# A reciprocal of 16 softmax denominators leaves the step that transposes them and becomes a step of its own

## The chip, the cores and the metric

The kernel runs on one core of a Trainium2 chip. The metric is the device time of one execution in microseconds (us), the median of several runs.

## The reference

One inference step of a two-layer decoder trunk, for a prompt of 1024 tokens and a sample group of 8 x 4 tokens that share the weights. Layer 0 projects its input once and feeds two mixers: a gated depthwise convolution of width 31, and attention with 16 heads of 64. Layer 1 is a gated linear recurrence. In the prompt's attention a head attends under three (window, dilation) pairs, and the three outputs are merged by their softmax denominators:

```python
DSWA_CONFIGS = ((128, 1), (512, 4), (2048, 16))
...
    scores = jnp.where(mask[None, None, :, None, :, :], scores, -jnp.inf)
    lse = jax.nn.logsumexp(scores, axis=-1)
    p = jnp.exp(scores - lse[..., None])
    o = jnp.einsum('ndbhqk,ndbkhe->ndbqhe', p.astype(vv.dtype), vv)
...
def dswa_merge(parts):
    outs = jnp.stack([o for o, _ in parts], axis=0).astype(jnp.float32)
    lses = jnp.stack([l for _, l in parts], axis=0)
    w = jax.nn.softmax(lses, axis=0)
    return jnp.einsum('cnth,cnthe->nthe', w, outs)
```

That merge equals one softmax over all keys, each counted as often as the three windows hold it. The kernel computes it so: a mask adds the logarithm of the count, one exponential is taken, its sum over the keys is the denominator, and the output is divided by it at the end.

## The kernel before

The program is generated by a planner written in Python that emits every engine's instructions in an order of its own and holds a clock for each engine (`clk`). The spine is a list of dense jobs (`dense`): each multiplies one 128-column block of a weight with all tokens in three chunks of 384, 384 and 288, in fp32 split into high and low halves, 24 matmuls for a chunk. They go into three PSUM tiles named d, and VectorE or ScalarE evacuates them.

All other work is in threads, lists of atoms (steps). An atom has an engine ("kind"), a set of keys that it depends on, a key that it sets when it ends, and a claim on buffers. A thread's atoms are issued strictly in their order. After every three dense matmuls `sides()` goes through the threads by priority (attention has 2, the convolution's taps 5) and issues what may go. For a TensorE atom the planned end of all that it depends on must lie 300 ns back (LEAD), a PSUM tile x must be free, and neither ScalarE's nor VectorE's planned clock may be more than 1500 ns ahead of TensorE's. For an atom of another engine that engine's planned clock may be at most 800 ns ahead (QUEUE):

```python
                if a.kind == "pe":
                    ok = r <= now + LEAD and self.xrel[0] <= now + 60 and max(c["act"], c["dve"]) <= now + 1500
                else:
                    ok = r <= max(now, c[a.kind]) + 60 and c[a.kind] <= now + QUEUE and (not a.bulk or c["dma"] <= now + 3000)
```

On the chip each engine works through its own queue in the order of issue and waits on semaphores.

`attention(pr)` makes the thread of one pair of heads, eight in all. For the blocks i = 0 to 7 of 128 queries: `qk(i)` multiplies (PSUM tiles x), a custom VectorE instruction adds the mask and finds the extreme, and ScalarE takes the exponential; its accumulated sums go into one column each of `den` (128 queries x 16, a column for each head and block). `tr` and `far` transpose the exponentials, `pv` and `far_pv` multiply with the values into PSUM tile o; `far_pv(1)` is the last of them, 32 matmuls and one copy by ScalarE into `S["o"]`. Then `fin1` takes the reciprocal of `den` on VectorE, transposes it on TensorE into 16 rows, and copies the rows out of PSUM on ScalarE; `fin2` and `fin3` write them to DRAM and read them back broadcast; `fin4` multiplies the output by them on GpSimd; `fin5` stores it for the gate.

Between a pair's `fin1` and the next pair's `qk(0)` lies a stretch of dense jobs alone. Beside attention, VectorE works on the 26 taps that it has of each of the 8 convolution blocks (scalar_tensor_tensor of 128x1024), on evacuations of d and x, and on the rotary additions. After attention, from 768 us on, come the decode attention over the cached keys and values (thread `dec`, whose bulk loads are paced by the planner's DMA clock), the layer norm and gates of layer 0, its output projection, and layer 1.

All calls go through a proxy, so the profile gives line 157 for nearly every instruction; they are told apart by engine, operation and form.

Of the kernel before, what the change touches and what calls it, by code (L numbers as in the profile page):

```python
# [176 lines left out]
class Kern:  # L177
# [786 lines left out]
    def attention(self, pr):  # L964
        nc, A = self.nc, self.A
        S = self.pair[pr]
# [116 lines left out]
        atoms = [Atom(store, "sp", [("rk", pr, c) for c in range(3)] + [("rq", pr, c) for c in range(3)], ("ko", pr))]  # L1083
        K = lambda n, i: (n, pr, i)
        for i in range(9):
# [3 lines left out]
            if i:  # L1089
# [5 lines left out]
                if t % 4 == 3:  # L1095
                    atoms.append(Atom(far_pv(t // 4), "pe", [K("pv", t)] + [K("far", x) for x in range(max(2, t - 3), t + 1)],
                                      K("fp", t // 4)))

        def fin1():
            den = S["den"]  # L1100
            nc.vector.reciprocal(den[:, :16], den[:, :16])
            p = self.px()
            nc.tensor.transpose(p[0:16, 0:128], den[:, :16], self.ident)
            S["d2"] = A.alloc(128)
            nc.scalar.copy(S["d2"][0:16, :].rearrange("p (a r) -> p r a", r=4),
                           p[0:16, 0:128].rearrange("p (r a) -> p r a", r=4))
            den.free()
            for n in ("q", "k", "vt", "vf"):
                S[n].free()
            if pr == NPAIR - 1:  # L1110
                self.mask.free()
# [15 lines left out]
        def fin5():  # L1127
            nc.sync.dma_start(self.ybd[pr][:, 0:T], S["o"].f)
            S["o"].free()
            self.fin["ob", pr] = self.clk["pe"] + 3000  # L1130

        atoms += [Atom(fin1, "pe", [("fp", pr, 1)], ("att", pr), (2, 0)), Atom(fin2, "sp"),
                  Atom(lambda: None, "sp"), Atom(fin3, "sp"), Atom(fin4, "pool"), Atom(fin5, "sp")]
        self.spawn(f"att{pr}", 2, atoms)

# [1482 lines left out]
```

## Time and profile before

| | us |
|---|---|
| median of 3 runs | 2374.55 |
| lowest and highest | 2374.27, 2379.08 |
| the profiled execution | 2373.09 |
| its span, from first to last instruction | 2371.2 |

| engine | busy us | share of the span |
|---|---|---|
| TensorE, matmuls (PE) | 2267.1 | 96% |
| TensorE, weight loads (PEld) | 2121.7 | 89% |
| VectorE (DVE) | 1617.8 | 68% |
| ScalarE (ACT) | 1025.2 | 43% |
| GpSimd (POOL) | 1055.1 | 44% |

The span is that of one execution under the hardware profiler; the profiled execution's own time is 1.9 us more. Weight loads overlap matmuls. Busy shares are averages over stages with different limits. The mean granted clock of TensorE is 0.985 of full speed.

### The profile page before, as it was taken

How to read it: one execution, taken by the hardware profiler on the slowest of the kernel's cores; microseconds unless marked ns; L12 is line 12 of the kernel's file. 1: busy time of each engine (PE TensorE's matmuls, PEld its weight loads, DVE VectorE, ACT ScalarE, POOL GpSimd, SP SyncE). 2: the span in 40 equal slices, each digit the busy share in tenths (PEclk: the TensorE clock that was granted, in tenths of full speed). 3: DMA queues.
4: the chain of work that ended last, by engine and by line, in shares of the span. 5: the costliest groups of instructions: out<-in, count | busy, mean ns of one | idle time of the engine just before them, and what ended most of it. 6: DMA issues, size and time to landing. Idle time of an engine off the chain costs nothing.

```text
span 2371.2 us, 42772 instructions
## 1 busy us (share of the span) xinstructions
PE 2267.1 (96%) x17387; PEld 2121.7 (89%) x17387; DVE 1617.8 (68%) x2466; ACT 1025.2 (43%) x1858; POOL 1055.1 (44%) x703
## 2 busy tenths in 40 slices
PE   7999999999989999999979999999999999999997
PEld 6987888887886798889969999999999999998996
DVE  7999988798786546752686666666666666667336
ACT  5454444444444322333445444444454444444332
POOL 4655555465454323434553333333333333345436
PEclk9999999999999999999989999999999999999998
DMA  4131221221235867874441111111211222232525
GB/s 151 54 95 40 77 75 40 77 75 40 77 114 210 336 246 294 296 268 138 142 165 51 67 64 64 64 64 64 73 58 64 73 73 73 74 101 98 176 96 175
DMA packets 118173, 271.60 MB, mean 115 GB/s; under 512 B 32336, under 2 KB 59472, under 8 KB 117968
## 3 DMA queue, kind: packets, MB, share of 16 engines
q1 hardware_dynamic: 117968, 268.78, 33.2%
q8 instruction: 139, 2.28, 0.4%
q14 instruction: 66, 0.54, 0.1%
HBM read 215.00 MB, written 53.73 MB: 113 GB/s over the span
## 4 chain that ended last, share of the span: by engine, by line
PE 73%; DVE 15%; issue 4%; ACT 3%; POOL 2%; DMA 2%; SPq 0%; DVEq 0%; POOLq 0%; ACTq 0%
PE d L157 41%; PE x L157 31%; DVE b L157 14%; ACT b L157 3%; POOL b L157 2%; PE o L157 1%; DVE c L157 1%; ACT c L157 0%; DMA b<-yd 0%; DMA b<-ybd 0%; DMA b<-rd 0%; DMA b<-wab 0%; SPq L157 0%; DMA b<-kc 0%; POOL c L157 0%
## 5 line engine op out<-in xcount | busy, mean ns | idle before, releaser
L157 PE MATMUL d<-c,b 128*128 128x384 f32 (+1 forms) x7896 | 1396.6, 331 | 22.1 <-ACT b L157 10.9
L157 PEld LDWEIGHTS d<-c,b 128*128 128x128 f32 x7896 | 1288.2, 190 | 69.6 <-issue 39.7
L157 POOL TENSOR_TENSOR b<-b,b 128x1024 fp32r<-128x1024 f32 (+6 forms) x422 | 845.8, 2015 | 860.8 <-ACT b L157 675.3
L157 ACT ACTIVATE b<-b 128x384 f32<-128x384 f32 (+14 forms) x647 | 357.0, 567 | 822.7 <-DVE b L157 809.9
L157 PE MATMUL x<-c,b 128*128 128x384 f32 (+4 forms) x3640 | 583.1, 311 | 26.2 <-DVE b L157 21.3
L157 PEld LDWEIGHTS x<-c,b 128*128 128x128 f32 (+2 forms) x3640 | 541.5, 175 | 43.9 <-issue 19.8
L157 DVE SCALAR_TENSOR_TENSOR b<-b,c,b 128x1024 f32<-128x1024 f32 (+2 forms) x258 | 406.5, 1578 | 10.9 <-ACT b L157 8.3
L157 DVE TENSOR_TENSOR b<-b,b 128x384 f32<-128x384 f32 (+14 forms) x297 | 303.4, 1035 | 89.8 <-ACT b L157 66.6
L157 PE MATMUL x<-b,b 128*32 128x128 f32 (+12 forms) x4528 | 281.9, 339 | 5.1 <-POOL b L157 4.3
L157 DVE SCALAR_TENSOR_TENSOR b<-b,b 128x384 f32<-128x384 f32 (+3 forms) x216 | 198.3, 924 | 107.0 <-ACT b L157 105.4
L157 PEld LDWEIGHTS x<-b,b 64*32 64x32 f32 (+3 forms) x4528 | 201.1, 127 | 56.8 <-issue 39.4
L157 DVE TENSOR_TENSOR b<-d,b 128x384 f32<-128x384 f32 (+3 forms) x278 | 139.9, 510 | 156.1 <-PE d L157 147.6
L157 ACT CAST b<-b 128x1024 fp32r<-128x1024 f32 (+3 forms) x264 | 224.7, 862 | 33.2 <-DMA b<-od 8.4
L157 DVE TENSOR_TENSOR b<-x,b 128x384 f32<-128x384 f32 (+3 forms) x162 | 81.9, 506 | 134.0 <-PE x L157 119.0
L157 POOL TENSOR_SCALAR b<-b 128x32 f32<-128x32 f32 x40 | 31.3, 782 | 288.1 <-DVE b L157 282.7
L157 ACT COPY b<-x 128x512 f32<-128x512 f32 (+4 forms) x177 | 86.4, 498 | 147.7 <-PE x L157 130.1
L157 DVE COPY b<-x 128x512 f32<-128x512 f32 (+8 forms) x216 | 100.5, 476 | 71.8 <-PE x L157 60.3
L157 ACT COPY b<-d 32x384 f32<-32x384 f32 (+2 forms) x212 | 94.7, 447 | 123.7 <-DVE b L157 80.6
L157 DVE CUSTOM_DVE_ANT_0 b<-x,b 128x128 f32<-128x128 f32 (+8 forms) x144 | 72.0, 532 | 51.9 <-PE x L157 47.7
L157 ACT ACTIVATE b<-b,c 128x512 f32<-128x512 f32 (+1 forms) x112 | 94.8, 875 | 2.6 <-DVE b L157 0.5
L157 POOL TENSOR_TENSOR b<-b,c 128x248 f32<-128x248 f32 (+1 forms) x48 | 66.8, 1406 | 36.2 <-PE d L157 33.2
L157 POOL COPY b<-b 128x32 f32<-128x32 f32 (+1 forms) x105 | 54.4, 528 | 47.8 <-DVE b L157 45.9
(59 smaller groups left out, 937.9 us busy)
## 6 DMA issues: line engine op xcount, KB each, us to landing
b<-wc SPq DMA_DIRECT2D x64, 512.0 KB, 4.2
b<-wab SPq DMA_DIRECT2D x56, 512.0 KB, 5.8
b<-kc SPq DMA_DIRECT2D x64, 448.0 KB, 6.5
b<-vc SPq DMA_DIRECT2D x64, 448.0 KB, 8.3
b<-woa SPq DMA_DIRECT2D x32, 512.0 KB, 4.2
b<-woc SPq DMA_DIRECT2D x32, 512.0 KB, 4.2
b<-yd SPq DMA_DIRECT2D x16, 528.0 KB, 6.2
ybd<-b SPq DMA_DIRECT2D x16, 512.0 KB, 3.0
```

The source lines that it names most:

```text
L157: r = f(*a, **k)
```

## The change

The reciprocal leaves `fin1` and becomes `fin0`, an atom of kind "dve". It depends on the end of `qk(7)`, stands in the thread after `far_pv(1)` and ahead of `fin1`, and sets a key that `fin1` now needs as well:

```diff
+        def fin0():
+            nc.vector.reciprocal(S["den"][:, :16], S["den"][:, :16])
+
         def fin1():
             den = S["den"]
-            nc.vector.reciprocal(den[:, :16], den[:, :16])
             p = self.px()
             nc.tensor.transpose(p[0:16, 0:128], den[:, :16], self.ident)
...
-        atoms += [Atom(fin1, "pe", [("fp", pr, 1)], ("att", pr), (2, 0)), Atom(fin2, "sp"),
+        atoms += [Atom(fin0, "dve", [("qk", pr, 7)], ("den", pr)),
+                  Atom(fin1, "pe", [("fp", pr, 1), ("den", pr)], ("att", pr), (2, 0)), Atom(fin2, "sp"),
                   Atom(lambda: None, "sp"), Atom(fin3, "sp"), Atom(fin4, "pool"), Atom(fin5, "sp")]
```

The planner's clocks see the two steps at other times than the one before, so the order of later instructions may differ too.

## Rows read from the trace of the kernel before

**Rows 1.** The page: span, and busy us, share and instructions of TensorE.

```profile
span 2371.2 us, 42772 instructions
...
PE 2267.1 (96%) x17387; PEld 2121.7 (89%) x17387; DVE 1617.8 (68%) x2466; ACT 1025.2 (43%) x1858; POOL 1055.1 (44%) x703
```

**Rows 2.** Windows: length, busy us (instructions) of PE PEld DVE ACT POOL, clock, DMA share.

```profile
66.00:768.30 702.30, 666.48 (x6150) 577.48 (x6148) 605.52 (x835) 319.05 (x698) 383.53 (x236) 0.99 0.26 80
...
235.40:330.79 95.39, 90.86 (x807) 80.45 (x808) 91.81 (x115) 43.92 (x97) 48.06 (x31) 1.00 0.21 60
330.79:421.58 90.79, 87.42 (x773) 76.96 (x774) 77.92 (x106) 41.40 (x92) 53.81 (x32) 0.98 0.22 63
421.58:507.38 85.80, 80.47 (x738) 69.77 (x739) 72.09 (x99) 36.99 (x82) 42.69 (x27) 1.00 0.23 66
507.38:596.67 89.29, 85.90 (x773) 75.42 (x774) 78.18 (x106) 41.39 (x92) 55.06 (x32) 1.00 0.21 64
596.67:682.54 85.87, 80.35 (x737) 69.64 (x738) 72.05 (x99) 37.01 (x82) 42.91 (x27) 1.00 0.22 66
```

**Rows 3.** TensorE's waits from 66 to 768.5 us: total, times, longest.

```profile
PE x L157 <- DVE b L157: 18.0, 14, 3.1
PE o L157 <- DVE b L157: 6.0, 10, 1.2
```

**Rows 4.** Groups by form, whole span: busy, mean ns, idle before, releasers.

```profile
L157 PE MATMUL x<-c,b 128*16 128x128 f32 x8 | 2.2, 269 | 14.8 <-DVE b L157 14.8
...
L157 PE MATMUL o<-b,b 128*64 128x128 f32 x608 | 49.1, 284 | 10.4 <-DVE b L157 6.0 <-ACT b L157 4.4
```

**Rows 5.** Timeline at the third pair's transpose: start, us, instruction [idle before].

```profile
321.88 1.71 PE L157 MATMUL o<-b,b 128*64 128x128 f32 x32
...
323.14 2.59 DVE L157 SCALAR_TENSOR_TENSOR b<-b,c,b 128x1024 f32<-128x1024 f32 x2
...
323.51 4.21 PE L157 MATMUL d<-c,b 128*128 128x384 f32 x27
...
326.65 1.63 DVE L157 TENSOR_TENSOR b<-b,b 128x384 f32<-128x384 f32 x1 [0.92 <-POOL b L157]
328.20 0.54 DVE L157 TENSOR_TENSOR b<-d,b 128x384 f32<-128x384 f32 x1
328.67 1.81 DVE L157 SCALAR_TENSOR_TENSOR b<-b,c,b 128x1024 f32<-128x1024 f32 x1
...
330.40 0.24 DVE L157 RECIPROCAL b<-b 128x16 f32<-128x16 f32 x1
...
330.79 0.27 PE L157 MATMUL x<-c,b 128*16 128x128 f32 x1 [3.06 <-DVE b L157]
330.81 9.25 PE L157 MATMUL d<-c,b 128*128 128x288 f32 x44
```

**Rows 6.** Timeline at the fourth pair's transpose.

```profile
415.80 3.44 DVE L157 SCALAR_TENSOR_TENSOR b<-b,c,b 128x1024 f32<-128x1024 f32 x2
...
421.58 0.27 PE L157 MATMUL x<-c,b 128*16 128x128 f32 x1 [1.61 <-DVE b L157]
```

**Rows 7.** Windows after the long waits, and the timeline after the fifth pair's.

```profile
330.81:335.01 4.20, 4.20 (x18) 4.20 (x19) 4.16 (x4) 1.72 (x5) 4.07 (x2) 0.59 0.20 62
682.57:686.77 4.20, 4.20 (x18) 4.20 (x19) 4.16 (x4) 1.72 (x5) 4.07 (x2) 0.59 0.16 58
507.40:511.60 4.20, 4.20 (x26) 4.20 (x27) 4.16 (x4) 1.71 (x5) 4.09 (x2) 1.00 0.19 66
...
507.38 0.27 PE L157 MATMUL x<-c,b 128*16 128x128 f32 x1 [2.99 <-DVE b L157]
507.40 9.28 PE L157 MATMUL d<-c,b 128*128 128x288 f32 x53
```

**Rows 8.** The decode stage: its window, and GpSimd's waits for loads of values there.

```profile
768.30:1060.00 291.70, 281.21 (x2589) 247.67 (x2590) 175.05 (x315) 94.14 (x163) 98.89 (x94) 0.98 0.77 285
...
POOL b L157 <- DMA b<-vc: 10.4, 1, 10.4
```

## The prediction

> **What bounds the kernel now.** I read the page first, then the windows, then the waits of TensorE, then the timelines of the places where the change acts. The page gives a span of 2371.2 us with TensorE busy for 2267.1 of it [rows 1]. So what counts is time in which TensorE stands still or runs at a lower clock; other engines count only where they hold it up. The profiled execution took 2373.09 us, 1.9 more than its span and 1.5 less than the median of the three runs, 2374.55; what I take off the one I take off the other.
>
> The change sits in attention, which runs from 66 to 768 us. In that stretch TensorE is busy 666.48 of 702.30 us, so it idles 35.8 us; VectorE is busy 605.52, which is 86% [rows 2]. Of TensorE's idle time, 18.0 us are waits of x matmuls (attention's PSUM tiles) for VectorE, in 14 waits of up to 3.1 us [rows 3]. The instructions by form show whose they are: the transpose of the 128x16 denominators, run eight times, once for each pair of heads, has 14.8 us of idle time before it, all put down to VectorE [rows 4], while the reciprocal that it waits for takes 0.24 us [rows 5]. The wait is therefore hardly the reciprocal; it is the place of the reciprocal in VectorE's queue.
>
> The timeline of the third pair shows this. TensorE finishes the last attention matmuls (32 of them, from 321.88), does 27 dense matmuls from 323.51 to 327.72, and then stands for 3.06 us, until the transpose at 330.79. VectorE meanwhile works through two taps of the convolution (323.14 to 325.73), a rotary addition, a PSUM evacuation and one more tap; only then, at 330.40, comes the reciprocal [rows 5]. Its input, the sums of the exponentials, is ready long before: the transposes of the last exponentials, and all that is made of them, lie ahead of the 32 matmuls.
>
> **The change part by part.** It takes the reciprocal out of fin1 and makes it a step of its own, fin0, which the planner may issue on VectorE as soon as the thread has come to it, that is right after far_pv(1) (those 32 matmuls). fin1 still waits for far_pv's copy by ScalarE, and now for fin0 too. It adds no instruction and no DMA: eight reciprocals of 0.24 us before, eight after, and eight transposes. On the queues of SP and POOL nothing is passed; the stores and loads of fin2 to fin5 follow fin1 as before.
>
> *The wait that goes.* If the reciprocal is issued after far_pv(1), it stands on VectorE behind what was issued up to then. For the third pair that is at worst the two taps that end at 325.73, so it is done by 325.97, and TensorE comes to the transpose at 327.72: 1.75 us to spare. The narrowest of the eight is the pair whose transpose starts at 421.58: two taps end at 419.24, the reciprocal would end at 419.48, and TensorE was ready at 421.58 - 1.61 = 419.97 [rows 6], with 0.49 to spare; the pair at 596.67 repeats this order. So up to 14.8 us go.
>
> *What stays of it.* The trace doesn't show a transpose whose reciprocal was issued ahead. From below the price is nothing. From above it is 0.6 us for each, the mean of the ten waits of matmuls into o for VectorE (6.0 us in all [rows 3]): 8 x 0.6 = 4.8. The nearest row is that of the o matmuls, whose operands are copied by separately issued steps, with the planner's lead, just as the reciprocal's result will be: 10.4 us of idle [rows 4] over 8 pairs x 10 steps (8 pv, 2 far_pv), 0.13 us each. I take 0.13 for six pairs and 0.6 for the two narrow ones: 2.0 us. The removal is worth 14.8 - 2.0 = 12.8 us.
>
> *The clock.* After two of the three long waits TensorE's granted clock was 0.59 of full over the next 4.20 us, and 18 matmuls ran there; after the third, 2.99 us long, it stayed at 1.00, and 26 ran [rows 7]. In the first 9.3 us after the wait that is 44 matmuls [rows 5] against 53 in 9.28 us [rows 7], of the same kind: nine fewer at 9.28/53 = 0.175 us, 1.6 us lost, twice: 3.2 us. With the waits this goes too. The bounds are 0, if a shorter wait elsewhere makes the clock fall instead, and 4.8, if the third wait costs as much in other executions. The Trainium skill (TensorE: Matmul & The Clock Gate, Part 1: The HAM clock gate) has the lower of the two levels as the default, which activity lifts and idleness brings back at a moment that varies from run to run. If every one of the eight waits had cost a spell like these two, the sum would hold 8 x 1.6 = 12.8 us for the clock instead of 3.2; the trace bears it out for two of eight, so I don't count on it.
>
> *Where the stall goes.* With TensorE some 3 us earlier, VectorE is as much later against it. What is due next from VectorE are evacuations of dense PSUM tiles, of which there are three (d). After the third and the fifth of the eight waits TensorE ran its dense matmuls for over 9 us without another (the rows of 9.25 us [rows 5] and 9.28 us [rows 7]), and the other six look alike. VectorE has the room to catch up, since it idles 96.8 us in the stretch (702.30 - 605.52 [rows 2]). If that cover were gone, the wait would reappear there (first rival).
>
> *The order of everything after.* The planner's clocks shift, so it will interleave differently from the first pair on. The rows let this be priced. Five successive pairs, from 235.40 to 682.54, stand in different orders; beside the wait at the transpose, TensorE idles in them 95.39 - 90.86 - 3.06 = 1.47, then 1.76, 2.34, 1.79 and 2.46 us [rows 2]. All at the highest would add 2.5 us, all at the lowest would save 2.5. Two pairs in one order (235.40 to 421.58, 186.2 us, 1580 matmuls) and two in another (421.58 to 596.67, 175.1 us, 1511 matmuls) differ by 69 matmuls, at 0.16 us some 11 us: the order moves work between windows and loses little. I take 0, with 2.5 either way.
>
> *The sum.* 14.8 - 2.0 + 3.2 + 0 = 16.0 us less: 2374.55 - 16.0 = 2358.5 us, a span of about 2355. With all bounds at one end it is 14.8 + 4.8 + 2.5 = 22.1 less (2352.5), at the other 14.8 - 4.8 - 2.5 = 7.5 less (2367).
>
> **The rivals.** *The wait moves on.* VectorE is behind when the reciprocal is late; an earlier transpose does not make it faster, and TensorE may meet the lateness at its next need. For it: in the window from 235.40 VectorE is busy 91.81 of 95.39 us, 96% [rows 2]. Against it: the 9 us without a wait after the transposes, and the other four windows, at 84 to 88%. If half of the removal comes back, 6.4 us, the time is 2374.55 - 9.6 = 2365.
>
> *The step isn't earlier.* The planner issues a VectorE step only when VectorE's planned clock is less than QUEUE (800) ahead of TensorE's. If VectorE is further ahead after far_pv(1) at each pair, fin0 slips behind the next tap, and if it slips as far as fin1, nothing changes: 2374.5. For it: in the third pair 27 dense matmuls and three VectorE instructions lie between, and some of these may be issued early. Against it: a convolution tap has the lower priority (5 against 2), so the first VectorE step issued when there is room is fin0.
>
> *The decode stage comes in a worse order.* From 768 to 1060 us the cached keys and values are loaded, the DMA engines are 77% busy, and TensorE idles 10.5 of 291.70 us; the longest wait for such a load there, GpSimd's, is 10.4 us [rows 8]. The stage begins earlier and is planned anew; if TensorE then waits for loads, it may lose more than attention gained. For it: the DMA share is the highest of the kernel there. Against it: the loads are issued relative to the same planned clocks, so the whole stage shifts with its start. It ends slower than no change from 16.0 + 4.7 = 20.7 us of new waits on; with the stage's idle time tripled (21 us more) the time is 2374.55 - 16.0 + 21 = 2379.5.
>
> **How the numbers follow.** A measurement of this kernel can tell about 0.2%, 4.7 us, from no change. I give my forecast 0.62, the wait that moves on 0.12 (0.10 of it faster, the rest within), the step that isn't earlier 0.08, the decode stage 0.18 (0.15 slower, 0.03 within). That makes faster 0.72, same 0.13, slower 0.15. The likeliest case has 2352.5 to 2367 as its own range. The range of 8 in 10 takes in the second and third cases: 2352 to 2375. The time predicted is the likeliest one's, 2358.5.
>
> **What would show it.** In the profile of the changed kernel: the eight transposes (128x128 into 16 rows) with under 3 us of idle before them in all; each reciprocal 0.5 us or more ahead of its transpose, and ahead of the tap that it follows now; no spell at about 0.6 of the clock right after a transpose; TensorE's idle time from 66 us to the last transpose down from 35.8 to some 23, and that transpose some 16 us earlier than 768.27; from there to the end the same time as before within 3 us. The prediction is wrong if the eight waits turn up at other x or o matmuls, if the reciprocal still stands right ahead of its transpose, or if the stages after 768 us grow by as much as attention shrinks.

## The result and the profile after

The changed kernel takes 2347.8 us (median of 5 runs, 2345.33 to 2350.76) against 2374.55; the ratio is 0.9891, 95% interval 0.988 to 0.9902. That is 26.7 us faster where 16.0 was forecast, and below the range of 2352 to 2375. The profiled execution has the median's time, 2347.8, with a span of 2344.8 us.

The page of the changed kernel, answering to [rows 1]:

```profile
span 2344.8 us, 42760 instructions
...
PE 2256.7 (96%) x17387; PEld 2115.6 (90%) x17387; DVE 1615.1 (69%) x2465; ACT 1023.7 (44%) x1856; POOL 1065.2 (45%) x706
```

TensorE is busy for 10.4 us less with the same 17387 matmuls, where the prediction's sum had 3.2 (its clock term). The instructions of VectorE, ScalarE and GpSimd number 2465, 1856 and 706 against 2466, 1858 and 703: the planner also picks the engine of some copies and additions by its clocks, so what is called an order below includes such moves. Its groups by form, answering to [rows 4]:

```profile
L157 PE MATMUL x<-c,b 128*16 128x128 f32 x8 | 2.2, 271 | 0.2
...
L157 PE MATMUL o<-b,b 128*64 128x128 f32 x608 | 49.1, 284 | 11.7 <-DVE b L157 9.6 <-ACT b L157 1.9
```

The transposes' idle time fell from 14.8 to 0.2 us; that of the o matmuls is about as before (10.4). Its timeline at the third pair, answering to [rows 5]:

```profile
310.20 1.71 PE L157 MATMUL o<-b,b 128*64 128x128 f32 x32
...
311.75 0.24 DVE L157 RECIPROCAL b<-b 128x16 f32<-128x16 f32 x1
311.83 1.46 PE L157 MATMUL d<-c,b 128*128 128x288 f32 x9
...
313.14 0.27 PE L157 MATMUL x<-c,b 128*16 128x128 f32 x1
```

In this pair the reciprocal now ends 1.15 us ahead of its transpose, and only 9 dense matmuls lie between the last attention matmuls and the transpose, where there were 27. So the planner issued fin1 sooner here; which of its conditions made the difference is not shown.

To compare stages, a point with equal work behind it is needed. At the start of layer 1 both kernels have a matmul that waits 9.4 or 9.5 us for VectorE (1217.24 us before, 1190.19 after). The windows from 66 us to there, first of the kernel before, then of the changed one:

```profile
66.00:1217.24 1151.24, 1095.16 (x9667) 971.22 (x9665) 865.22 (x1256) 476.54 (x964) 568.22 (x377) 0.99 0.42 144
```

```profile
66.00:1190.19 1124.19, 1084.92 (x9668) 965.07 (x9666) 861.11 (x1255) 475.18 (x962) 578.24 (x380) 0.99 0.43 147
```

All of the gain, 27.05 us, lies ahead of this point; after it the changed kernel takes 0.7 us more (2344.8 - 1190.19 against 2371.2 - 1217.24). TensorE's idle time fell from 56.08 to 39.27, by 16.8 us, and its busy time from 1095.16 to 1084.92, by 10.2. Of the idle time 14.6 us are the eight waits, and a net 2.2 other waits.

In these two executions the busy time shrank mostly through the clock. These are the windows in that stretch in which the granted clock was 0.50, that is 1.2 GHz, first of the kernel before, then of the changed one:

```profile
331.50:334.90 3.40, 3.40 (x13) 3.40 (x12) 3.36 (x4) 1.22 (x3) 3.38 (x2) 0.50 0.19 66
683.10:686.50 3.40, 3.40 (x13) 3.40 (x13) 3.36 (x4) 1.21 (x4) 3.40 (x2) 0.50 0.15 55
710.40:717.20 6.80, 4.97 (x29) 2.71 (x30) 3.22 (x8) 0.49 (x1) 1.87 (x5) 0.50 1.00 380
816.20:823.00 6.80, 6.04 (x20) 4.97 (x24) 4.18 (x7) 1.08 (x1) 1.29 (x1) 0.50 1.00 392
993.70:1000.50 6.80, 5.19 (x16) 3.77 (x20) 5.65 (x5) 1.35 (x4) 3.53 (x2) 0.50 0.31 103
```

```profile
691.20:698.00 6.80, 3.98 (x26) 1.72 (x27) 3.71 (x6) 0.00 (x0) 2.64 (x4) 0.50 0.00 0
786.80:790.10 3.30, 3.30 (x26) 1.31 (x19) 1.67 (x5) 1.50 (x2) 1.55 (x1) 0.50 0.86 270
978.00:981.30 3.30, 3.30 (x18) 2.08 (x20) 3.27 (x5) 0.48 (x1) 3.30 (x3) 0.50 0.00 0
```

The first two spells of before follow the long waits at the transposes ([rows 7]) and are gone. The other three follow waits elsewhere, and where there were three of 6.8 us there are now one of 6.8 and two of 3.3. In all 27.2 us at half clock became 13.4; at half speed each us there costs half, so at most 13.8 / 2 = 6.9 us came from the clock (less where TensorE idled within a spell). At least 3.3 us of the busy time are not explained here.

The clock's part is not a fixed number. Over the 48 executions of the kernel before that were timed beside the experiments the mean granted clock is 0.984 to 0.988, on average 0.9861; over the five of the changed kernel it is 0.985 to 0.988, on average 0.9868. With mean spans of 2372 and 2346 us this makes (1 - 0.9861) x 2372 - (1 - 0.9868) x 2346 = 2.0 us, as an estimate, while the two profiled executions, at 0.985 and 0.987, differ by 5 in the same sum. By this estimate the clock's part in the gain of the medians is smaller than in this pair of traces.

### The profile page after: what moved, and what is told of

The parts are those of the page before. It is cut to its first block, busy times and chain, and to the rows that moved or that the text cites. A ratio compares the mean times of both kernels' runs of the same rounds, so it can differ in the third digit from the quotient of the medians.

```text
span 2344.8 us, 42760 instructions
## 1 busy us (share of the span) xinstructions
PE 2256.7 (96%) x17387; PEld 2115.6 (90%) x17387; DVE 1615.1 (69%) x2465; ACT 1023.7 (44%) x1856; POOL 1065.2 (45%) x706
## 4 chain that ended last, share of the span: by engine, by line
PE 63%; DVE 3%; DMA 2%; ACT 1%; POOL 1%; issue 1%; SPq 0%; POOLq 0%; DVEq 0%; ACTq 0%
PE d L157 33%; PE x L157 29%; DVE b L157 3%; ACT b L157 1%; DMA b<-vc 1%; POOL b L157 1%; DVE c L157 1%; DMA b<-ybd 1%; PE o L157 0%; DMA b<-kc 0%; SPq L157 0%; DMA b<-x1d 0%; ACT c L157 0%; POOL c L157 0%; ACT L157 0%
## 5 line engine op out<-in xcount | busy, mean ns | idle before, releaser
L157 POOL TENSOR_TENSOR b<-b,b 128x1024 fp32r<-128x1024 f32 (+7 forms) x423 | 854.1, 2031 | 827.5 <-ACT b L157 616.6
L157 DVE TENSOR_TENSOR b<-b,b 128x384 f32<-128x384 f32 (+13 forms) x296 | 312.7, 1072 | 85.7 <-ACT b L157 69.9
L157 DVE SCALAR_TENSOR_TENSOR b<-b,b 128x384 f32<-128x384 f32 (+3 forms) x216 | 193.2, 898 | 111.4 <-ACT b L157 103.2
L157 DVE COPY b<-x 128x512 f32<-128x512 f32 (+6 forms) x217 | 101.5, 479 | 77.3 <-PE x L157 70.1
```

Of the source, the lines that this page charges most:

```text
L157: r = f(*a, **k)
```

## The experiments

Each was compared with the kernel before, run on the same chip beside it. Three theories stood at first: that the waits and the half-clock spells behind them are the whole gain (wait theory); that a better order of everything after made it (order theory); both, added up.

**e1 and e2: the place of the reciprocal and the planned order, each alone.** The planner's clocks and the emitted instruction can be separated: `account` moves the clocks without an instruction, `real` emits one past the clocks. e1 has the order of the kernel before on TensorE, ScalarE, GpSimd and SyncE, instruction for instruction; on VectorE only the reciprocal has moved. e2 is the reverse, with the order of the changed kernel.

```diff
 # e1, on the kernel before: in far_pv, behind its copy
+                if G == 1:
+                    nc.vector.real.reciprocal(S["den"][:, :16], S["den"][:, :16])
...
 # in fin1
-            nc.vector.reciprocal(den[:, :16], den[:, :16])
+            self.fill("dve")
+            self.account("dve", "reciprocal", (den[:, :16], den[:, :16]), {})
...
 # e2, on the changed kernel: in fin0
-            nc.vector.reciprocal(S["den"][:, :16], S["den"][:, :16])
+            self.fill("dve")
+            self.account("dve", "reciprocal", (S["den"][:, :16], S["den"][:, :16]), {})
...
 # in fin1
+            nc.vector.real.reciprocal(den[:, :16], den[:, :16])
```

> The order of the kernel before on every engine; only the reciprocal moves, on VectorE's queue to right behind far_pv(1)'s copy, unseen by the planner (its clocks count it in fin1 as before). Wait theory (the eight waits and the half-clock spells behind two of them are the whole gain): the time of the changed kernel, 2348 us, with the transposes' idle time at 0. Order theory (the waits only move on; a better order made the gain): the time of the kernel before, 2374. Both (what the two traces add up to: 14.6 us of waits and 3.4 of clock by the place, the other 9 by the order): 2356.

> The order of the changed kernel on every engine; only the reciprocal moves back, to right ahead of its transpose, while the planner's clocks count it in fin0. Wait theory: the waits come back, 2363 to 2375 us. Order theory: 2348, no change from the changed kernel. Both: 2358 to 2366, with 10 to 15 us of idle time at the transposes.

Measured: e1 2367.84 us, ratio 0.9972 (0.9963 to 0.9981); e2 2367.18, ratio 0.9965 (0.9952 to 0.9979). As ratios to the kernel before:

| | reciprocal late | reciprocal early |
|---|---|---|
| order of before | 1 | 0.9972 |
| order of the changed kernel | 0.9965 | 0.9891 |

All three theories failed, the sum too (e2 alone would suit the wait theory, but e1 doesn't). Each part alone gives about 0.3%, 7 to 8 us; together they give 1.1%, where the product of the two would be 0.9937. The group of the transposes in e1 and then in e2 shows that the waits were moved as meant:

```profile
L157 PE MATMUL x<-c,b 128*16 128x128 f32 x8 | 2.2, 272 | 0.0
```

```profile
L157 PE MATMUL x<-c,b 128*16 128x128 f32 x8 | 2.2, 271 | 15.6 <-DVE b L1105 15.6
```

In e1 a part of the waits came up again later. The timeline at the fifth pair's first transposes of exponentials, 23 us after the fourth pair's transpose in the kernel before (421.58 us) and 24.5 us after it in e1 (412.20 us); the kernel before, then e1:

```profile
433.15 1.67 DVE L157 TENSOR_TENSOR b<-b,b 128x384 f32<-128x384 f32 x1 [3.26 <-POOL b L157]
...
444.57 0.71 PE L157 MATMUL x<-c,b 128*128 128x128 f32 x2 [1.52 <-ACT b L157]
```

```profile
425.40 1.65 DVE L157 TENSOR_TENSOR b<-b,b 128x384 f32<-128x384 f32 x1 [3.75 <-POOL b L157]
...
436.75 0.85 PE L157 MATMUL x<-c,b 128*128 128x128 f32 x2 [3.06 <-ACT b L157]
```

TensorE comes to the fourth transpose without its wait of 1.61 us, but VectorE takes up the rotary step 13.2 us after the transpose where it was 11.6, having stood for GpSimd (3.75 us, 3.26 before). The exponentials of the next pair come as much later, and TensorE's wait of 1.52 us there becomes 3.06, with a half-clock spell behind it (its window, from 437.30 us on, stands below). In all, TensorE idles 26.4 us from 66 us to the last transpose in e1 (691.17 - 664.78, below), against 35.8 before, so a net 5.4 of the 14.8 us came up again; the profiled execution of e1 took 2363.21 us, 4.6 less than e1's median, so more is lost in most of its executions. The prediction's first rival, the wait that moves on, is thus a part of what happens in the old order. Why less in the new one?

**e3, e4, e7 and e8: other orders.** Four kernels that only make the planner choose another order: e3 puts fin0 right behind qk(7); e4 is the kernel before and e7 the changed one with the planner's price of a reciprocal 50 ns higher (`6 * n + 180` for `6 * n + 130`); e8 is the changed one with `LEAD = -290`. What was expected of e7 and e8 names two more theories: that the gain comes whole only if the planner no longer counts on a stall that is gone (belief theory), and that the changed kernel's order just happens to be a good one (chance theory).

```diff
 # e3, on the changed kernel
-        atoms += [Atom(fin0, "dve", [("qk", pr, 7)], ("den", pr)),
-                  Atom(fin1, "pe", [("fp", pr, 1), ("den", pr)], ("att", pr), (2, 0)), Atom(fin2, "sp"),
+        n = next(i for i, x in enumerate(atoms) if x.key == ("tr", pr, 7))
+        atoms.insert(n, Atom(fin0, "dve", [("qk", pr, 7)], ("den", pr)))
+        atoms += [Atom(fin1, "pe", [("fp", pr, 1), ("den", pr)], ("att", pr), (2, 0)), Atom(fin2, "sp"),
```

> fin0 stands in the thread right behind qk(7), so the reciprocal is issued several us earlier still; the order of everything after is planned anew. Wait theory: nothing more to gain, 2348 within 1 us. Order theory, and both: whatever the new order costs or gives, 2340 to 2357, with no waits at the transposes.

> The kernel before; only the planner's price of a reciprocal is 50 ns higher, so that it plans another order with the reciprocal in its old place. Wait theory: 2374 within 3 us, waits of 12 to 17 us at the transposes. Order theory: the time moves by up to 10 us either way though the waits stay.

> The changed kernel; only the planner's price of a reciprocal is 50 ns higher, so another order is planned. Belief theory: 2348 within 5 us, no wait at the transposes. Chance theory: 5 to 15 us slower, since the changed kernel's order was a lucky one.

> The changed kernel; only LEAD is 290 instead of 300 ns, for yet another order. Belief theory: 2348 within 5 us, no wait at the transposes. Chance theory: 5 to 15 us slower.

Measured: e3 2352.9 us, ratio 0.9914 (0.9901 to 0.9927); e4 2373.77, 0.9996 (0.9986 to 1.0006); e7 2360.41, 0.9942 (0.9929 to 0.9955); e8 2352.42, 0.9907 (0.9893 to 0.9921). With the reciprocal in its old place and its stall counted there, another order gives nothing (e4, with 14.0 us of waits at the transposes); the order of e2, planned without the stall, gave 8 us with the reciprocal in the same place. With fin0 the order is worth up to 12 us (e7 against the changed kernel), so e7 lies outside the range of the belief theory (2348 within 5 us) and inside that of the chance theory; e8 lies within the former. An earlier place than the changed kernel's gains no more (e3).

**e5, e6, e10 and e11: does the planner count on a stall?** In the kernel before, and so in e1, the planner's clock of TensorE jumps at fin1 to the end of the reciprocal, and all that the planner then issues on the other engines is paced by that clock. In the changed kernel it doesn't. e5 is e1 without the two lines in fin1, so the clocks count the reciprocal nowhere. e6 is the changed kernel with those two lines added in fin1, so a stall is counted that isn't there. e10 and e11 are e1 and e5 with `LEAD = -290`.

> The reciprocal right behind far_pv(1)'s copy as in e1, but the planner's clocks count it nowhere, so they hold no stall of TensorE at fin1 and an order without one is planned. Belief theory (the gain comes whole only if the planner no longer counts on a stall that is gone): near the changed kernel, 2345 to 2355 us, though the step fin0 isn't there. Chance theory (the changed kernel's order happens to be a good one): anywhere from 2350 to 2370, as for any other order.

> The changed kernel, reciprocal early in fin0, but the planner's clocks count a second reciprocal in fin1, with TensorE waiting for it; none is issued there. Belief theory: like e1, 2360 to 2370 us, with waits of 1.5 to 3 us at the first transposes of exponentials of a pair or elsewhere in attention. Chance theory: anywhere from 2345 to 2370; if it is near 2348, a believed stall costs nothing.

> e1 (early reciprocal, planner still counts it in fin1) with LEAD at 290 ns, so another order with a believed stall. Belief theory: in attention, from 66 us to the last transpose, idle time of TensorE above 24 us, and a time of 2362 us or more. Chance theory: as likely below 2358 as above.

> e5 (early reciprocal, counted nowhere) with LEAD at 290 ns, so another order without a believed stall. Belief theory: idle time of TensorE in attention below 24 us, 2345 to 2358 us. Chance theory: as likely above 2360 as below.

Measured: e5 2350.28 us, ratio 0.9902 (0.9888 to 0.9916); e6 2369.54, 0.9976 (0.9967 to 0.9984); e10 2362.98, 0.9954 (0.994 to 0.9967); e11 2358.89, 0.9933 (0.992 to 0.9947). At the transposes they wait 0.7 us in all (e11) or not at all. The first three of these times are as the belief theory had them; e11 lies 0.9 us above its range. All kernels with an early reciprocal, by what the planner counts:

| stall counted in fin1 | ratio | no stall counted | ratio |
|---|---|---|---|
| e1 | 0.9972 | changed kernel | 0.9891 |
| e6 | 0.9976 | e5 | 0.9902 |
| e10 | 0.9954 | e8 | 0.9907 |
| | | e3 | 0.9914 |
| | | e11 | 0.9933 |
| | | e7 | 0.9942 |
| mean | 0.9967 | mean | 0.9915 |

No ratio of one group lies within the other, but the intervals of e7 and e11 overlap that of e10. In attention the separation is plainer. These are the windows from 66 us to the last transpose in e1, e6, e10, and then e3, e8, e11; the six have run within ten matmuls of the kernel before at that point (6150 in 702.30 us [rows 2]):

```profile
66.00:757.17 691.17, 664.78 (x6140) 576.31 (x6138) 604.88 (x833) 318.68 (x698) 386.56 (x236) 0.99 0.26 81
```

```profile
66.00:761.88 695.88, 666.68 (x6147) 576.87 (x6146) 609.49 (x832) 319.25 (x699) 390.32 (x237) 0.99 0.26 81
```

```profile
66.00:762.39 696.39, 667.89 (x6144) 579.17 (x6144) 607.71 (x834) 318.57 (x698) 385.79 (x236) 0.99 0.27 81
```

```profile
66.00:748.19 682.19, 659.92 (x6144) 572.18 (x6143) 609.87 (x835) 318.14 (x697) 378.91 (x235) 0.99 0.27 82
```

```profile
66.00:750.54 684.54, 662.68 (x6145) 575.11 (x6144) 611.48 (x834) 318.48 (x699) 379.87 (x235) 0.99 0.27 82
```

```profile
66.00:752.69 686.69, 662.30 (x6149) 573.83 (x6147) 613.15 (x834) 318.37 (x697) 380.00 (x237) 0.99 0.27 82
```

For the same work the first three take 691 to 696 us, the last three 682 to 687. A stall that is counted but gone costs attention some 10 us of the 16 to 20 that its removal gives there. Half of the 10 is idle time of TensorE (on average 28.0 us against 22.8), half busy time (666.5 against 661.6). The waits from 66 to 750 us show where, for e1, e6, e10, and then the changed kernel and e8:

```profile
DVE b L157 <- POOL b L157: 18.3, 15, 3.7
...
PE x L157 <- ACT b L157: 6.3, 4, 3.1
```

```profile
DVE b L157 <- POOL b L157: 17.7, 13, 4.6
...
PE x L157 <- ACT b L157: 8.2, 5, 3.8
```

```profile
DVE b L157 <- POOL b L157: 19.2, 15, 4.6
...
PE x L157 <- ACT b L157: 7.1, 4, 3.9
```

```profile
DVE b L157 <- POOL b L157: 8.3, 10, 2.2
```

```profile
DVE b L157 <- POOL b L157: 6.9, 8, 2.2
...
PE x L157 <- ACT b L157: 0.3, 1, 0.3
```

TensorE's waits for ScalarE, which makes the exponentials, are 6.3 to 8.2 us where the stall is counted; in the changed kernel and e7 there are none, in e3, e5, e8 and e11 0.3 to 2.5 us, in the kernel before 3.5. The two longest of each of e1, e6 and e10 stand at the first transposes of exponentials of the fifth and the seventh pair, as in e1 above, and a spell at half clock follows each. In e1 the waits are 3.06 and 2.70 us (at 436.75 and 609.71 us), and these the windows behind them; in e10 the waits are 3.89 and 2.77 us, with 6 us at 0.50 behind each.

```profile
437.30:440.60 3.30, 3.30 (x14) 3.30 (x15) 3.01 (x9) 1.44 (x6) 0.00 (x0) 0.50 0.02 5
611.30:614.60 3.30, 3.30 (x13) 3.30 (x12) 2.91 (x7) 2.19 (x7) 0.00 (x0) 0.50 0.03 5
```

VectorE's waits for GpSimd are about twice as long where the stall is counted (in e3, e5, e7 and e11 they are 8.5 to 12.7 us, in the kernel before 14.4). So most of what the counted stall costs are waits for exponentials and the clock behind them. That the counted stall itself makes the planner hand more to GpSimd ahead of the rotary steps is argued from this, not shown.

**e9: one more wait removed.** In the changed kernel the longest wait in attention is 6.3 us, of the first decode matmuls for GpSimd, which itself waits for VectorE with the halving of the sample tokens' gates. e9 puts the halving on VectorE.

```diff
-            self.halve(self.gs[:, pr * NS:pr * NS + NS], S["g"][:, T:NTOK])
+            nc.vector.tensor_scalar(self.gs[:, pr * NS:pr * NS + NS], S["g"][:, T:NTOK], 0.5, None, op0=OP.mult)
```

> The changed kernel, with the halving of the sample tokens' gates of layer 0 (128x32, once for each pair) on VectorE instead of GpSimd, where in the changed kernel it waits for VectorE and holds back the blocks that the first decode matmuls need (TensorE idles 6.3 us there, with a half-clock spell). If that wait goes and the order is as good: 2336 to 2342. If another order eats it: 2345 to 2355.

Measured: 2348.28 us, ratio 0.9888 (0.9873 to 0.9904), no different from the changed kernel. The windows from 66 us to the last transpose, of the changed kernel and of e9:

```profile
66.00:755.75 689.75, 668.65 (x6210) 579.61 (x6209) 608.64 (x849) 318.76 (x699) 381.45 (x238) 1.00 0.28 87
```

```profile
66.00:761.82 695.82, 680.16 (x6327) 589.18 (x6325) 612.95 (x861) 322.81 (x706) 388.02 (x242) 1.00 0.29 92
```

The wait went, and idle time in attention fell from 21.1 to 15.7 us, but at the start of layer 1 e9 is only 2.8 us ahead (1187.42 against 1190.19): by then TensorE has idled 5.7 us less, and has been busy 2.9 us more with as many matmuls. Why it is busy longer wasn't settled, and the medians don't show the 2.8 us. No version beat the changed kernel.

## Why the prediction was wrong

**The wait that goes.** Right: the eight waits were VectorE's queue, not the reciprocal, and they are gone. The reciprocals end 0.15 us or more ahead of their transposes; the 0.5 that was to be seen is missed at two of them, without a wait.

**What stays of it.** Taken as 2.0 us; it is 0.2. The bound of nothing was the right one, and for the place alone: e1, with the transposes planned as before, has 0.0.

**The clock.** The two spells behind the transposes went, as priced (3.2 us). But spells elsewhere shrank as well: in this pair of traces up to 6.9 us came back, and the term counted only the spells that follow the transposes. Over all executions the estimate is 2.0 us, nearer to the 3.2 that were priced, so this term is not what failed.

**The order of everything after.** This is the step that failed: "I take 0, with 2.5 either way". The bound was read from five windows of one plan, all of them with a planned stall, and so it said nothing of plans without one. The runs put the new order alone, the waits still there, at 0.9965 (e2, about 8 us), and the early reciprocal without it at 0.9972 (e1, about 7 us). The 16.0 forecast for the removal isn't to be had by the removal alone; it takes the order planned for it, and then the two give more than their sum. The removal was priced as if the rest stayed as it was; in the old order more than half of the 16.0 is lost again, and e1's trace shows a net 5.4 us of that as other waits. Six orders without a counted stall average 0.9915, some 20 us, inside the prediction's range; the changed kernel's is the best of the six, and that part, about 6 us, is a lucky order.

**The rivals.** The wait that moves on is real, above all where the planner still counts the stall (e1, e6, e10). In the changed kernel a little of it shows too: from 66 to 750 us the o matmuls wait 9.6 us for VectorE (6.0 before) and the first decode matmuls 6.3 us for GpSimd (3.8 before), but the 3.5 us of waits for ScalarE are gone. The step that isn't earlier occurred at two of the eight pairs, where the reciprocal still stands right ahead of its transpose; but the transpose came later as well, and nothing waits. The fourth pair's:

```profile
402.69 0.23 DVE L157 RECIPROCAL b<-b 128x16 f32<-128x16 f32 x1
...
403.07 0.27 PE L157 MATMUL x<-c,b 128*16 128x128 f32 x1
```

The decode stage came in a slightly better order here, and in e7 in a worse one, which made most of its 12 us. The windows from the last transpose on, of the changed kernel and of e7, with the same work:

```profile
755.75:1056.10 300.35, 291.99 (x2661) 262.61 (x2659) 174.23 (x312) 104.25 (x179) 123.92 (x105) 0.99 0.78 285
```

```profile
757.25:1067.80 310.55, 296.99 (x2662) 264.56 (x2660) 182.85 (x316) 104.02 (x178) 113.43 (x103) 0.98 0.76 276
```

They differ by 10.2 us, half of it idle time. So a worse order of that stage costs 10 us here, and not the 21 that the third rival needed. That the loads are the cause, as that rival had it, is not shown: GpSimd's longest wait for a load of values there is 11.4 us in e7, but it was 10.4 in the kernel before too [rows 8].

**What was to be seen.** TensorE's idle time up to the last transpose is 21.1 us (some 23 expected). That transpose comes 12.5 us earlier, not 16, and from there to the end the time is 13.9 us shorter, not the same; with 60 more matmuls done by then (6210, against 6150 [rows 2]), some 10 us of this are work that moved ahead of it.

What stays open: which of the planner's decisions the counted stall spoils, where e9's gain went, and what made TensorE's busy time shrink beside the clock.

## What to carry to other kernels

A small instruction that one engine needs from another should be issued ahead of the step that consumes it, early enough to come through the other engine's queue; still earlier gained nothing more here (e3). Where a planner lays out the order, the gain is whole only if its model loses the stall too: moving the instruction while the planner went on counting it in its old place gave a quarter of it (e1), and without counting it nearly all (e5). And a re-planned order is a term of its own, here up to 12 us between orders that differ by a parameter of 10 or 50 ns, so one kernel's time says little of a change until a few other orders have been run.

## What the hardware showed

The length of a wait alone doesn't say whether the clock falls. A wait of 2.99 us left it at 1.00 [rows 7], while in e2 one of 1.86 us was followed by a window at 0.50:

```profile
589.38 0.27 PE L157 MATMUL x<-c,b 128*16 128x128 f32 x1 [1.86 <-DVE b L1105]
```

```profile
590.30:593.60 3.30, 3.30 (x16) 3.30 (x15) 2.65 (x3) 1.72 (x4) 0.00 (x0) 0.50 0.24 51
```

The Trainium skill (TensorE: Matmul & The Clock Gate, Part 1: The HAM clock gate) says that the moment of the change varies from run to run; by that rule the same waits can cost differently in two executions. The two rows can't show this, since they are different waits in two kernels; what agrees with it is the mean granted clock of the kernel before, 0.984 to 0.988 over its 48 executions.
